# Two-layer diffusion backbone with mixture of experts: the last four expert tiles of layer 0 summed on chip, and the loop over further tiles moved to three tiles from the end

## The chip, the cores and the metric

The kernel runs on one core of one Trainium2 chip. The metric is device time in microseconds (us), the median over runs of one program. The engines are named as in the profile: PE (TensorE, its matmuls), PEld (its weight loads), DVE (VectorE), ACT (ScalarE), POOL (GpSimd), SP (SyncE, which only issues transfers here).

## What is computed

Two layers over 256 latent tokens and 256 context tokens of 1024 numbers each. A layer makes modulation vectors from the conditioning, projects, runs three kinds of attention, projects out, and adds the result with a scaled residual and a layer norm. Then comes the mixture of experts: 32 experts in 4 groups, each token takes the two best experts of its best group:

```python
    out = jnp.zeros_like(h)
    for e in range(N_EXPERTS):
        hidden = jax.nn.silu(h @ w1[e]) * (h @ w3[e])
        out = out + combine[..., e:e + 1] * (hidden @ w2[e])
    return out
...
        x = _ln_affine(ALPHA * x + g2 * _hier_moe(h, w_rg[l], b_rg[l], w_re[l], b_re[l], w1[l], w3[l], w2[l]),
                       ln2_g[l], ln2_b[l])
```

Layer 0 does this for latents and context (512 tokens), layer 1 for the latents alone (256), and its latents are the output.

## The kernel before

**Blocks and tiles.** Tokens lie in blocks of 128 on the partitions: b0 and b1 are the latents, b2 and b3 the context. The experts' work is cut into tiles of 128 token slots: two experts with 64 slots each, or four with 32. Layer 0 has 14 tiles (t0 to t13), layer 1 has 12 (t0 to t11). An expert's weights are three chunks (c = 0, 1, 2) of 1 MiB; the first two hold w1 and w3, the last w2.

**A tile's steps.** `gather` brings the tokens of a tile together by one-hot matmuls (L1179); `up` multiplies by w1 and w3 (L1192), ACT and DVE make the gated product (L1198, L1199); `mid` turns it (L1226). What follows depends on the tile. An away tile does `put`: multiply by w2 (L1237) and write the 128 rows to the HBM tensor `ys` by an SP transfer of 512 KiB. A tile on chip does `back` (L1210 to L1218: which token a slot belongs to, with what weight), `down` (multiply by w2, L1250, evicted at L1258 and L1259, or L1254 to L1256 in layer 1) and `combine` (one-hot matmuls, L1273, added into one accumulator per block by DVE, L1278). In layer 0 the tiles t0 to t12 are away and t13 is on chip; in layer 1 all are on chip.

**The end of layer 0.** After the last `up`, `fold` reads the two rows of every token back from `ys` (8 indirect POOL transfers of 512 KiB, L1465), weighs and adds them (ACT L1469, DVE L1470), multiplies by the gate (L1471) and adds the residual (L1472). Then t13's `combine` is added, and the layer norm (`before`, L414 to L436) and layer 1's projections (L455 to L457, after the transposes L481) follow.

**Weights.** Expert weights come by `dyn_load` (POOL, L142), an indirect transfer that POOL issues; the other loads are issued by SP (L161). `pump` issues the stream's next loads while fewer than `cap` units of 1 MiB are held; a unit comes free when a step has read its chunk. POOL's transfers use eight semaphores in turn (DMASW0 to 7), SP's use eight others (DMAHW0 to 7).

**The loop over further tiles.** A group with more tokens than its slots hold is finished by `rest` (L1478, L1479), a loop on the device whose count `lpi` is read at run time. With these inputs the count is zero in both layers. RP = (1, 1) puts it after the last tile of each layer.

```python
            r = nc.values_load(lpi[0:1, 0:1], min_val=0, max_val=32)
            with tc.For_i(0, r, 1):
```

**Fillers.** The modulation weights of the next layer are multiplied in small steps (`mod_steps`, L320, four matmuls a step), put by `fill` into places where PE would wait; 16 of them belong to layer 1, four at its head, before the transposes, and the others inside its attention.

Of the kernel before, what the change touches and what calls it, by code (L numbers as in the profile page):

```python
# [35 lines left out]
LAG = 2  # L36
FA = (0, 0, 0, 3)
AC = (5, 8)
RP = (1, 1)
LC = (4, 12)  # L40


class Mem:
# [74 lines left out]
def backbone(ctx: ExitStack, tc, ins, out):  # L118
# [64 lines left out]
    def stream_chunk(k, l, c):  # L183
        add((k, l, c), ins["w_in_" + k][l, c], 4 * CH[k])
# [63 lines left out]
    stream_mod(1, 1, 0, 4)  # L248
    for c in range(2):
        stream_chunk("kc", 1, c)  # L250
    for c in range(2, 5):
        stream_b(1, c)
    stream_mod(1, 1, 4, 8)
    for c in range(2):
        stream_chunk("v", 1, c)
    add(("sm", 1), ins["w_small"][1], 1888)
# [121 lines left out]
    def fill(n=1):  # L378
        for _ in range(n):
            if fillers:  # L380
                fillers.pop(0)()
# [77 lines left out]
    def layer(l, first, before=None, after=None):  # L459
        nb = 4 if l == 0 else 2  # L460
        nq = 128 * nb
        last = l == NL - 1
# [6 lines left out]
        tb = mem.get(512)  # L469
        ta = tb.v(2, 2, 2, 64)  # L470

        hT = [[mem.get(UNIT, F32R) for _ in range(2)] for _ in range(2)]
        HT = [[h.v(4, 512) for h in x] for x in hT]

        def turned(items):

# [784 lines left out]

        total = t3("total", 2, 2)

        def combine(par, first=False, final=0):

            OT = oht[par].v(nb, 128)
            YHI, YLO = parts()
            for b in range(nb):
                for f in range(2):
                    fs = slice(f * 512, f * 512 + 512)  # L1270
                    p = bank("a")
                    for i, Y in enumerate((YHI, YLO)):
                        PE.matmul(p, lhsT=OT[:, b, :], rhs=Y[:, f, :], start=(i == 0), stop=(i == 1))  # L1273
                    dst = ACC[b][:, fs]
                    if last and final:
                        V.scalar_tensor_tensor(dst, p, 1.0, dst, op0=OP.mult, op1=OP.add, accum_out=total[:, b, f:f + 1])
                    elif final == 1:
                        V.tensor_tensor(dst, p, BC["g2", b // 2][:, fs], OP.mult)  # L1278
                    elif final:
                        w = scratch()  # L1280
                        V.tensor_tensor(w, p, BC["g2", b // 2][:, fs], OP.mult)
                        V.tensor_tensor(dst, dst, w, OP.add)
                    elif first and not last:
                        S.activation(dst, p, AF.Copy)
                    else:
                        V.tensor_tensor(dst, dst, p, OP.add)

# [167 lines left out]
            for t in range(0 if last else 2):  # L1455
                mod_bcast(l, 5, t, BC["g2", t])

        def fold():

            two = [mem.get(D) for _ in range(nb)]  # L1460
            for b in range(nb):
                acc[b] = mem.get(D)
                ACC[b] = acc[b].v(D)
                for dst, j in ((ACC[b], 0), (two[b].v(D), 1)):
                    G.indirect_dma_start(out=dst, out_offset=None, in_=ys[:, :],  # L1465
                                         in_offset=bass.IndirectOffsetOnAxis(ap=find[:, b, j:j + 1], axis=0),
                                         bounds_check=at_row, oob_is_err=False)
# [5 lines left out]
            for k in two:  # L1473
                k.free()

        def rest(dyn, par, final):

            r = nc.values_load(lpi[0:1, 0:1], min_val=0, max_val=32)  # L1478
            with tc.For_i(0, r, 1):  # L1479
                further(35)  # L1480

                def load(c):
                    if c < 3:
                        dyn_load(dyn, idx[:, NE, c:c + 1])

                load(0)
                onehot(par, [(128, 35)])
                for jj in range(0, 8, 2):
                    gather(par, 1, jj)
                hb = up(par, 0, 1, 128, lambda t, c: dyn, lambda c: load(c + 1))  # L1490
                ws = back(par, 0, 1, 128, 35, par)
                down(mid(hb), ws, 128, lambda t, c: dyn, lambda c: None)
                combine(par, False, final)

        at_rest = len(todo) - RP[l]
        for i, (m, col, e, _, go) in enumerate(todo):
# [11 lines left out]

            def others():
                held = [("exp", l, e + t, 2) for t in range(128 // m)]  # L1510
                rest(slot[held[0]], i % 2 if i < len(todo) - 1 else 0, 2 if i == len(todo) - 1 else 0)
                for k in held:
                    drop(k)
                pump()

            if i == len(todo) - 4:
                cap[0] -= 2
            if i == len(todo) - 1:
                cap[0] = LC[l]
            if i == len(todo) - 2:  # L1520
                xg.pop((qe + 1) % 2).free()
                ohs.pop((qe + 1) % 2).free()
# [12 lines left out]
            hc = None if i < away else mid(hb)  # L1535
            if q < qe:
                for jj in range(4 * at_, 4 * at_ + 4, 2):
                    gather(q + 1, len(sets[q + 1]), jj)
            if i < away:
                put(i, mid(hb), m, W, rel)  # L1540
# [9 lines left out]
        for k in split_y + [iw] + xg + ohs + oht + hh:  # L1550
            k.free()
        cap[0] = 5


        def second(b, xn):
            xn[b] = mem.get(D) if last else acc[b]
            yield from deepnorm(X[b], xn[b].v(D), BC["lg"], BC["lb"], last, 1.0, total[:, b] if last else None)
            if last:
                SP.dma_start(out=out[b * 128:(b + 1) * 128, :], in_=X[b])

        def done():
            for k in bc.values():
                k.free()

        return second, done
# [6 lines left out]
    before, after = layer(0, mod0_steps(0, "e"))  # L1572
    for g in (1, 2):
        fillers.extend(mod_steps(1, g))
    before, after = layer(1, None, before, after)
    together(*[before(b, {}) for b in range(2)])


# [86 lines left out]
```

## Time and profile before

| | before |
|---|---|
| median of 3 runs | 1125.83 us (1125.26 to 1126.35) |
| the profiled execution | 1121.56 us |
| its span in the profile | 1119.8 us |
| PE busy | 1000.2 us, 89% of the span |
| DVE busy | 510.2 us, 46% |
| DMA | 301.06 MB, mean 269 GB/s |
| mean granted PE clock | 0.96 of full speed |

The busy share of PE is a mean over stages. The two expert stages (450 to 607 us in layer 0, 900 to 1096 us in layer 1) move 411 to 420 GB/s, where the highest slice of the page has 423, while PE is nearly full too; between the expert stage of layer 0 and the projections of layer 1 (616 to 656 us) DVE works and PE mostly waits.

### The profile page before, as it was taken

The numbers are of one execution on the slowest core, as the hardware profiler recorded it, in microseconds if no ns is written. First come the engines' busy times: TensorE is split into PE (matmuls) and PEld (weight loads), VectorE is DVE, ScalarE is ACT, GpSimd is POOL, SyncE is SP. The second block draws the span as 40 slices with busy tenths as digits, with TensorE's granted clock in tenths as the row PEclk, the third lists the DMA queues.
The fourth block names the chain that finished last, engine by engine and source line by source line (L and its number), as shares of the span: only waits on it lengthen the run. The fifth ranks groups of instructions, "written<-read, shape, count | busy, mean of one in ns | idle before, by whom it ended". The sixth has DMA issues, their size and how long they took to land. (4 is left out here: it accounts for less than half of the span.)

```text
span 1119.8 us, 14771 instructions
## 1 busy us (share of the span) xinstructions
PE 1000.2 (89%) x5497; PEld 567.9 (51%) x5497; DVE 510.2 (46%) x1369; ACT 347.3 (31%) x707; POOL 303.3 (27%) x326
## 2 busy tenths in 40 slices
PE   4999999999999998999867279999998899999893
PEld 2788744557765553453212158854456554433231
DVE  5644367775575210100001887356665654342244
ACT  4533155553442110111000376134454221211011
POOL 2112134340002412434421222133210045443420
PEclk9999999999999999999999579999998799999997
DMA  9722157420469987899998563356425799999992
GB/s 381 304 73 91 43 207 285 176 76 1 170 272 364 421 357 299 354 422 423 421 421 351 215 221 119 112 201 241 165 76 225 286 363 419 421 421 421 421 421 95
DMA packets 46351, 301.06 MB, mean 269 GB/s; under 512 B 5410, under 2 KB 5794, under 8 KB 14532
## 3 DMA queue, kind: packets, MB, share of 16 engines
q0 software_dynamic: 25824, 177.81, 38.9%
q1 hardware_dynamic: 20452, 122.27, 28.8%
q8 instruction: 45, 0.74, 0.3%
q14 instruction: 30, 0.25, 0.1%
HBM read 292.19 MB, written 7.87 MB: 268 GB/s over the span
## 5 line engine op out<-in xcount | busy, mean ns | idle before, releaser
L142 POOL DMA_INDIRECT u<-in_w_exp,u x162 | 162.0, 1000 | 327.1 <-PE psa L1192 144.0
L1192 PE MATMUL psa<-u,u 128*32 128x512 f32 (+2 forms) x1040 | 221.3, 603 | 16.3 <-DMA u<-in_w_exp,u 16.2
L455 PE MATMUL psa<-u,u 128*128 128x512 f32 (+3 forms) x400 | 141.3, 356 | 1.0 <-ACT u L498 0.7
L456 PE MATMUL psa<-u,u 128*128 128x512 f32 (+3 forms) x400 | 140.4, 352 | 2.0 <-DVE u L450 2.0
L1192 PEld LDWEIGHTS psa<-u,u 128*32 128x32 f32 (+2 forms) x1040 | 65.5, 127 | 146.9 <-issue 109.9
L457 PE MATMUL psa<-u,u 128*128 128x512 f32 (+3 forms) x400 | 139.5, 352 | 0.4 <-DVE u L499 0.3
L1199 DVE TENSOR_TENSOR scr<-scr,psa 128x256 f32<-128x256 f32 x26 | 10.9, 420 | 213.1 <-ACT scr L1198 213.1
L1179 PEld LDWEIGHTS psc<-u,u 128*128 128x128 f32 x640 | 82.7, 197 | 31.5 <-issue 26.5
L878 POOL TENSOR_SCALAR u<-u,ri 128x512 f32<-128x512 f32 (+1 forms) x48 | 68.5, 1431 | 100.2 <-DVE ri L876 82.6
L1179 PE MATMUL psc<-u,u 128*128 128x256 f32 x640 | 92.7, 296 | 3.0 <-DVE u L1165 2.1
L455 PEld LDWEIGHTS psa<-u,u 128*128 128x128 f32 x400 | 75.7, 190 | 12.5 <-ACT u L498 1.1
L456 PEld LDWEIGHTS psa<-u,u 128*128 128x128 f32 x400 | 76.1, 190 | 11.7 <-DVE u L450 3.1
L457 PEld LDWEIGHTS psa<-u,u 128*128 128x128 f32 x400 | 75.6, 190 | 10.0 <-DVE u L499 0.9
L875 ACT ACTIVATE u<-psa,nm 128x512 f32<-128x512 f32 (+1 forms) x96 | 58.4, 615 | 55.8 <-DVE nm L873 50.9
L1198 ACT ACTIVATE scr<-psa 128x256 f32<-128x256 f32 x26 | 10.0, 385 | 192.1 <-PE psa L1192 192.1
L450 DVE TENSOR_TENSOR u<-u,u 128x1024 fp32r<-128x1024 f32 (+4 forms) x38 | 56.2, 1485 | 19.7 <-ACT u L449 19.6
L1237 PE MATMUL pse<-u,scr 128*32 128x512 f32 (+2 forms) x248 | 63.0, 600 | 1.9 <-ACT scr L1227 1.9
L1181 ACT ACTIVATE u<-psc 128x512 f32<-128x512 f32 x52 | 31.1, 597 | 107.9 <-PE psc L1179 69.4
L1250 PE MATMUL pse<-u,scr 128*64 128x512 f32 (+1 forms) x272 | 63.6, 599 | 0.6 <-DMA u<-in_w_exp,u 0.6
L873 DVE TENSOR_REDUCE nm<-psa 128x1 f32<-128x512 f32 (+1 forms) x80 | 53.1, 682 | 14.1 <-PE psa L863 10.5
L419 POOL TENSOR_TENSOR lns<-lns,mhalf 128x1 f32<-128x1 f32 x22 | 14.2, 646 | 149.0 <-DVE lns L418 108.3
L1273 PE MATMUL psa<-u,u 128*128 128x512 f32 x112 | 38.4, 458 | 17.1 <-DVE u L1278 11.0
(315 smaller groups left out, 1360.3 us busy)
## 6 DMA issues: line engine op xcount, KB each, us to landing
u<-in_w_mod SPq DMA_DIRECT2D x48, 1024.0 KB, 5.9
u<-in_w_exp SPq DMA_DIRECT2D x30, 1024.0 KB, 8.0
u<-in_w_out SPq DMA_DIRECT2D x8, 1024.0 KB, 5.0
ys<-u SPq DMA_DIRECT2D x13, 512.0 KB, 8.3
u<-in_w_in_b SPq DMA_DIRECT2D x10, 512.0 KB, 12.4
u<-in_w_in_v SPq DMA_DIRECT2D x4, 960.0 KB, 4.5
u<-in_w_in_qa SPq DMA_DIRECT2D x4, 768.0 KB, 10.4
u<-in_ln_rows SPq DMA_DIRECT2D x6, 512.0 KB, 5.8
```

The costliest lines, as they stand in the source:

```text
L142: G.indirect_dma_start(out=b.ap(UNIT), out_offset=None, in_=wexp_rows, in_offset=bass.IndirectOffsetOnAxis(ap=idx, axis=0), bounds_check=N ...
L450: V.tensor_tensor(l_[:, c], w[:, c], h[:, c].bitcast(F32), OP.subtract)
L455: PE.matmul(p, lhsT=a[0], rhs=b[0], start=first, stop=False)
L456: PE.matmul(p, lhsT=a[0], rhs=b[1], start=False, stop=False)
L457: PE.matmul(p, lhsT=a[1], rhs=b[0], start=False, stop=final)
L873: V.tensor_reduce(out=nm[:, s, 0:n], in_=pv, axis=AX.X, op=OP.max, negate=True)
L875: S.activation(P[:, i, :], pv[:, i, :], AF.Exp, bias=nm[:, s, i:i + 1], accum_out=su[:, s, i:i + 1])
L878: (G if s == 0 else V).tensor_scalar(P[:, i, :], P[:, i, :], ri[:, s, i:i + 1], None, op0=OP.mult)
L1179: PE.matmul(pv[:, j, :], lhsT=H[b][:, k * 128:(k + 1) * 128], rhs=OH[:, b, :], start=(b == 0 and i == 0), stop=(b == nb - 1 and i == 1))
L1192: PE.matmul(g[r, :], lhsT=XG[:, k, at * 128 + r.start:at * 128 + r.stop], rhs=W(t, k // 4).v(4, 512)[:, k % 4, :], start=(k == 0), stop=(k ...
L1237: PE.matmul(y[r, :], lhsT=hc[:, c * 128 + r.start:c * 128 + r.stop], rhs=W(t, 2).v(2, D)[:, c, f * 512:f * 512 + 512], start=(c == 0), sto ...
L1250: PE.matmul(y[r, :], lhsT=hc[:, c * 128 + r.start:c * 128 + r.stop], rhs=W(t, 2).v(2, D)[:, c, f * 512:f * 512 + 512], start=(c == 0), sto ...
```

## The change

HOME = 4 leaves 10 tiles away, so that t10 to t13 of layer 0 do `back`, `down` and `combine`. Reading back is cut in three: `fetch` (the 8 reads) after t10's `up`, `weigh` (weigh and add) after t11's, `fold` (gate and residual) after t13's. RP = (3, 3) puts the loop after t11 of layer 0's 14 tiles and after t9 of layer 1's 12; the tile ahead of it combines at once and keeps its w2 chunks through the loop. HC sets `cap`. The last `combine` is cut into the latents' half and the context's half, with the first step of the latents' layer norm between them. `mod(1,1)` is streamed earlier and eight of its steps stand at the head of layer 1 where there were four.

```diff
-RP = (1, 1)
-LC = (4, 12)
+RP = (3, 3)
+HOME = 4
+HC = (7, 9, 5)
...
-    for k in ("qa", "cq"):
-        for c in range(2):
-            stream_chunk(k, 1, c)
+    for c in range(2):
+        stream_chunk("qa", 1, c)
+    stream_mod(1, 1, 0, 4)
+    for c in range(2):
+        stream_chunk("cq", 1, c)
+    stream_mod(1, 1, 4, 8)
...
-            together(*[before(b, xn) for b in range(2)])
             for c in range(2):
                 presplit("qa", c)
-            fill(4)
+            rest_of([before(b, xn) for b in range(2)])
+            fill(5)
+            make_h()
+            fill(3)
...
-        away = 0 if last else len(todo) - 1
+        away = 0 if last else len(todo) - HOME
...
-        def fold():
-
-            two = [mem.get(D) for _ in range(nb)]
+        two = []
+
+        def fetch():
+
             for b in range(nb):
                 acc[b] = mem.get(D)
                 ACC[b] = acc[b].v(D)
+                two.append(mem.get(D))
                 for dst, j in ((ACC[b], 0), (two[b].v(D), 1)):
                     G.indirect_dma_start(out=dst, out_offset=None, in_=ys[:, :],
                                          in_offset=bass.IndirectOffsetOnAxis(ap=find[:, b, j:j + 1], axis=0),
                                          bounds_check=at_row, oob_is_err=False)
+
+        def weigh():
             for b in range(nb):
                 S.activation(ACC[b], ACC[b], AF.Copy, scale=sc_[:, b, 2:3])
                 V.scalar_tensor_tensor(ACC[b], two[b].v(D), sc_[:, b, 3:4], ACC[b], op0=OP.mult, op1=OP.add)
+            for k in two:
+                k.free()
+
+        def fold():
+
+            for b in range(nb):
                 V.tensor_tensor(ACC[b], ACC[b], BC["g2", b // 2], OP.mult)
                 V.scalar_tensor_tensor(X[b], X[b], ALPHA, ACC[b], op0=OP.mult, op1=OP.add)
...
+            if i == away - 2:
+                cap[0] = HC[0]
+            if last and i == len(todo) - 4:
                 cap[0] -= 2
...
             if i == len(todo) - 2:
...
                 rows()
+                cap[0] = HC[1]
+                pump()
...
-            if i and i - 1 != at_rest and i > away:
-                combine((i - 1) % 2, i == 1)
-            if i == len(todo) - 1 and not last:
+            if i == away and away:
                 for k in yo:
                     k.free()
+                fetch()
+            if i == away + 1 and away:
+                weigh()
+            if i > away and i - 1 != at_rest:
+                combine((i - 1) % 2)
+            if i == len(todo) - 1 and not last:
                 fold()
...
-            if i == at_rest and i < len(todo) - 1:
+            if i == at_rest:
                 combine(i % 2)
                 others()
-        combine((len(todo) - 1) % 2, False, 1)
-        if at_rest == len(todo) - 1:
-            others()
+        par = (len(todo) - 1) % 2
+        finish = [lambda b=b: combine(par, 1, range(b, b + 2)) for b in range(0, nb, 2)]
+        finish[0]()
```

**Where the loop stands on POOL, layer 1.** POOL issues the expert loads. Before, the end of its queue reads as follows: the last four expert loads, two rows of the layer norm's constants, and then the loop (its count is loaded, compared, and the body of three loads is jumped over).

```order
L142 DMA u_8395<-in_w_exp,u_6671 128x2048
L142 DMA u_8487<-in_w_exp,u_6671 128x2048
L142 DMA u_8491<-in_w_exp,u_6671 128x2048
L142 DMA u_8495<-in_w_exp,u_6671 128x2048
L1454 DMA u_8499<-in_ln_rows 128x1024 x2
L1478 TENSOR_LOAD lpi
L1479 COMPARE_AND_BRANCH
```

After the change, with the semaphores that each row waits for: four expert loads, the loop's count and first branch, then (left out here: the body) the row at which the loop is left, and three expert loads behind it.

```order
L143 DMA u_8518<-in_w_exp,u_6802 128x2048 [waits DMASW1_49,PE_49]
L143 DMA u_8522<-in_w_exp,u_6802 128x2048 [waits DMASW2_49,PE_49]
L143 DMA u_8526<-in_w_exp,u_6802 128x2048 [waits DMASW3_49,PE_49]
L1490 TENSOR_LOAD lpi [waits DVE_49]
L1491 COMPARE_AND_BRANCH
...
L1491 UNCONDITIONAL_BRANCH [waits DMASW5_49,DMASW4_49,DMASW6_49,DMASW3_49,DMASW7_49,DMASW2_49,DMAHW0_49,DMASW1_49,DMAHW1_49,DMASW0_49,DMAHW2_49,SP_sequencer_49,DMAHW3_49,DVE_sequencer_49,DMAHW4_49,PE_sequencer_49,DMAHW5_49,Activation_se
L143 DMA u_8795<-in_w_exp,u_6802 128x2048
L143 DMA u_8799<-in_w_exp,u_6802 128x2048
L143 DMA u_8803<-in_w_exp,u_6802 128x2048
L1458 DMA u_8807<-in_ln_rows 128x1024 x2
```

Three expert loads and the constants moved from ahead of the loop to behind it. The row at which the loop is left stands in the same words on all five queues, in both programs; a jump over the body leads there too, and the counts that it waits for are those of every transfer issued ahead of the loop (97 on POOL's eight semaphores in layer 0 of the changed kernel, the three of the body among them).

**Where it stands on PE, layer 1.** Before, the tail of PE's order is t11's last weights' multiplications, t11's `combine` and the loop:

```order
L1250 MATMUL pse<-u_8491,scr 64x512
L1250 MATMUL pse<-u_8495,scr 64x512
L1273 MATMUL psa<-u_6986,u_6987 128x512 x8
L1478 TENSOR_LOAD lpi
L1479 COMPARE_AND_BRANCH
```

After, t9's `down` and `combine` stand ahead of the loop, and all of t10's `up`, whose weights are u_8461 to u_8490, stands behind it:

```order
L1260 MATMUL pse<-u_8379,scr 32x512
L1260 MATMUL pse<-u_8457,scr 32x512
L1283 MATMUL psa<-u_7117,u_7118 128x512 x8
L1490 TENSOR_LOAD lpi
L1491 COMPARE_AND_BRANCH
...
L1491 REGISTER_ALU
L1491 COMPARE_AND_BRANCH
L1491 UNCONDITIONAL_BRANCH
L1202 MATMUL psa<-u_8461,u_7116 64x512
L1202 MATMUL psa<-u_8482,u_7116 64x512
```

Two whole tiles of PE's work (t10 and t11) moved behind the loop; in layer 0 it is t12 and t13.

**DVE at the end of layer 0.** Before, from the last tile's eviction to the loop, DVE weighs (L1470), gates (L1471), adds (L1472) and combines (L1278) in one run, of which this is the end:

```order
L1472 SCALAR_TENSOR_TENSOR u_72<-u_72,u_4713 128x1024
L1471 TENSOR_TENSOR u_4726<-u_4726,u_4611 128x1024
L1278 TENSOR_TENSOR u_4706<-psa,u_3034 128x512
L1472 SCALAR_TENSOR_TENSOR u_72<-u_72,u_4726 128x1024
L1278 TENSOR_TENSOR u_4713<-psa,u_3034 128x512 x2
L1278 TENSOR_TENSOR u_4713<-psa,u_4611 128x512 x2
L1278 TENSOR_TENSOR u_4726<-psa,u_4611 128x512 x2
L1478 TENSOR_LOAD lpi
```

After, between t13's gated product and the layer norm's first instruction (L427) stand t12's combine adds (L1290, eight, the last two shown), the gate and residual (L1485 and L1486, eight, three shown), and t13's combine of the latents:

```order
L1290 TENSOR_TENSOR u_4458<-u_4458,psa 128x512 x2
L1485 TENSOR_TENSOR u_4437<-u_4437,u_4451 128x1024
L1485 TENSOR_TENSOR u_4444<-u_4444,u_4451 128x1024
L1486 SCALAR_TENSOR_TENSOR u_71<-u_71,u_4437 128x1024
...
L1288 TENSOR_TENSOR u_4437<-psa,u_4451 128x512
L452 TENSOR_TENSOR u_5184<-u_4998,u_5183 128x512
L1288 TENSOR_TENSOR u_4437<-psa,u_4451 128x512
L1288 TENSOR_TENSOR u_4444<-psa,u_4451 128x512 x2
L452 TENSOR_TENSOR u_5192<-u_5040,u_5191 128x512 x3
L427 SCALAR_TENSOR_TENSOR u_71,dns<-u_71,u_4437 128x1024
```

The weighing, the loop and the context's combine left this stretch; eight combine adds and six splits of the projection's weights (L452, before: L450, inside the layer norm) came into it.

## Rows read from the trace of the kernel before

**Rows 1.** Windows: stretch, length, busy us (instructions) per engine, PEclk, DMA share, GB/s.

```profile
550.00:607.00 57.00, 42.06 (x151) 12.88 (x150) 5.01 (x15) 4.70 (x10) 11.88 (x12) 0.94 1.01 420
616.00:656.00 40.00, 14.25 (x41) 4.74 (x41) 34.17 (x59) 15.62 (x21) 11.88 (x14) 0.51 0.64 231
740.00:850.00 110.00, 106.54 (x535) 55.18 (x534) 72.82 (x149) 51.74 (x109) 29.43 (x24) 0.98 0.44 154
1064.00:1096.00 32.00, 29.82 (x126) 10.37 (x124) 11.66 (x20) 3.46 (x7) 6.43 (x8) 1.00 0.99 412
```

**Rows 2.** Timeline of POOL, layer 1's last issues: start, us, instruction [idle before, releaser].

```profile
1068.30 0.99 POOL L142 DMA_INDIRECT u<-in_w_exp,u  x1 [1.50 <-PE pse L1250]
1070.79 1.03 POOL L142 DMA_INDIRECT u<-in_w_exp,u  x1 [1.50 <-PE psa L1273]
...
1080.26 0.55 POOL L1454 DMA_DIRECT2D u<-in_ln_rows  x1 [1.65 <-DMA u<-in_w_exp,u]
```

**Rows 3.** Issues in 900 to 1064 us: count, median us to landing.

```profile
u<-in_w_exp,u POOLq DMA_INDIRECT x70, 19.1
```

**Rows 4.** Waits of SP's queue around layer 0's loop: total, times, longest.

```profile
SPq L1479 <- DVEq L1478: 6.2, 1, 6.2
```

**Rows 5.** Chain that ended last, at layer 1's loop: start, us, what.

```profile
1107.01 0.05 DVEq L1479
...
1108.29 0.23 DVE dns L427 x2
```

**Rows 6.** Timeline of DVE, end of layer 1: first instruction behind the loop.

```profile
1108.29 0.23 DVE L427 TENSOR_TENSOR dns<-total 128x1 f32<-128x1 f32 x2 [2.05 <-issue]
```

**Rows 7.** Timeline of DVE, end of layer 0.

```profile
619.91 1.22 DVE L1471 TENSOR_TENSOR u<-u,u 128x1024 f32<-128x1024 f32 x1
...
633.98 3.67 DVE L1278 TENSOR_TENSOR u<-psa,u 128x512 f32<-128x512 f32 x6
639.74 1.22 DVE L425 SCALAR_TENSOR_TENSOR u<-u,u 128x1024 f32<-128x1024 f32 x1 [2.08 <-issue]
...
644.74 0.68 DVE L450 TENSOR_TENSOR u<-u,u 128x512 fp32r<-128x512 f32 x1
```

**Rows 8.** Timeline of PE, last tiles of layer 1.

```profile
1072.37 7.08 PE L1192 MATMUL psa<-u,u 128*64 128x512 f32 x30
1080.38 0.44 PE L1226 MATMUL psa<-ident,scr 128*128 128x128 f32 x2 [0.93 <-DVE scr L1199]
1081.35 3.70 PE L1250 MATMUL pse<-u,scr 128*64 128x512 f32 x16
...
1086.50 2.29 PE L1273 MATMUL psa<-u,u 128*128 128x512 f32 x7 [0.21 <-DVE u L1256]
1088.71 7.08 PE L1192 MATMUL psa<-u,u 128*64 128x512 f32 x30
1096.72 0.44 PE L1226 MATMUL psa<-ident,scr 128*128 128x128 f32 x2 [0.93 <-DVE scr L1199]
```

**Rows 9.** Timeline of PE, `up` of t12 in layer 0.

```profile
581.92 5.34 PE L1192 MATMUL psa<-u,u 128*64 128x512 f32 x14 [2.73 <-DMA u<-in_w_exp,u]
```

**Rows 10.** Timeline of ACT, at the end of t13's `up` in layer 0.

```profile
607.19 0.38 ACT L1198 ACTIVATE scr<-psa 128x256 f32<-128x256 f32 x1 [14.58 <-PE psa L1192]
```

**Rows 11.** Timeline of PE: filler steps, first projection, broadcast of the gate.

```profile
529.35 2.21 PE L390 MATMUL psc<-u,ident 2*128 2x512 f32 x4
...
646.60 1.93 PE L320 MATMUL pse<-u,csil 128*32 128x512 f32 x8 [1.08 <-DMA u<-in_w_mod]
...
659.41 0.42 PE L455 MATMUL psa<-u,u 128*128 128x384 f32 x1
...
751.26 1.06 PE L320 MATMUL pse<-u,csil 128*32 128x512 f32 x8
```

**Rows 12.** Waits of PE in 740 to 850 us: total, times, longest.

```profile
PE pse L908 <- DVE u L897: 2.0, 5, 0.6
```

**Rows 13.** Page, transfers of SP: count, KB each, median us from issue to landing.

```profile
u<-in_w_mod SPq DMA_DIRECT2D x48, 1024.0 KB, 5.9
```

More of the change, by code (lines that the diff above doesn't have):

```diff
@@ L457, in three, with layer @@
         PE.matmul(p, lhsT=a[1], rhs=b[0], start=False, stop=final)
-    def layer(l, first, before=None, after=None):
+    def layer(l, first, before=None, after=None, rest_of=None):
         nb = 4 if l == 0 else 2
@@ L470, in layer, with make_h @@
         ta = tb.v(2, 2, 2, 64)
-        hT = [[mem.get(UNIT, F32R) for _ in range(2)] for _ in range(2)]
-        HT = [[h.v(4, 512) for h in x] for x in hT]
+        hT, HT = [], []
+        def make_h():
+            hT.extend([mem.get(UNIT, F32R) for _ in range(2)] for _ in range(2))
+            HT.extend([h.v(4, 512) for h in x] for x in hT)
+        if not last:
+            make_h()
         def turned(items):
@@ L744, in layer @@
             gains()
-            together(*[before(b, xn) for b in range(2)])
             for c in range(2):
                 presplit("qa", c)
-            fill(4)
+            rest_of([before(b, xn) for b in range(2)])
+            fill(5)
+            make_h()
+            fill(3)
             for j in range(0, 8, 2):
@@ L1262, in layer, with combine @@
         total = t3("total", 2, 2)
-        def combine(par, first=False, final=0):
+        def combine(par, final=0, blocks=range(nb)):
             OT = oht[par].v(nb, 128)
             YHI, YLO = parts()
-            for b in range(nb):
+            for b in blocks:
                 for f in range(2):
@@ L1276, in combine @@
                         V.scalar_tensor_tensor(dst, p, 1.0, dst, op0=OP.mult, op1=OP.add, accum_out=total[:, b, f:f + 1])
-                    elif final == 1:
+                    elif final:
                         V.tensor_tensor(dst, p, BC["g2", b // 2][:, fs], OP.mult)
[L1279 to L1284, printed above, removed]
                     else:
@@ L1470, in fold, with rest @@
                 V.scalar_tensor_tensor(ACC[b], two[b].v(D), sc_[:, b, 3:4], ACC[b], op0=OP.mult, op1=OP.add)
+            for k in two:
+                k.free()
+        def fold():
+            for b in range(nb):
                 V.tensor_tensor(ACC[b], ACC[b], BC["g2", b // 2], OP.mult)
                 V.scalar_tensor_tensor(X[b], X[b], ALPHA, ACC[b], op0=OP.mult, op1=OP.add)
-            for k in two:
-                k.free()
-        def rest(dyn, par, final):
+        def rest(dyn, par, odd):
             r = nc.values_load(lpi[0:1, 0:1], min_val=0, max_val=32)
@@ L1490, in rest @@
                 hb = up(par, 0, 1, 128, lambda t, c: dyn, lambda c: load(c + 1))
-                ws = back(par, 0, 1, 128, 35, par)
+                ws = back(par, 0, 1, 128, 35, odd)
                 down(mid(hb), ws, 128, lambda t, c: dyn, lambda c: None)
-                combine(par, False, final)
+                combine(odd)
         at_rest = len(todo) - RP[l]
@@ L1510, in others @@
                 held = [("exp", l, e + t, 2) for t in range(128 // m)]
-                rest(slot[held[0]], i % 2 if i < len(todo) - 1 else 0, 2 if i == len(todo) - 1 else 0)
+                rest(slot[held[0]], q % 2, i % 2)
                 for k in held:
@@ L1514, in others @@
                 pump()
-            if i == len(todo) - 4:
+            if i == away - 2:
+                cap[0] = HC[0]
+            if last and i == len(todo) - 4:
                 cap[0] -= 2
-            if i == len(todo) - 1:
-                cap[0] = LC[l]
             if i == len(todo) - 2:
-                xg.pop((qe + 1) % 2).free()
-                ohs.pop((qe + 1) % 2).free()
+                for k in hh + [xg.pop((qe + 1) % 2), ohs.pop((qe + 1) % 2)]:
+                    k.free()
                 rows()
+                cap[0] = HC[1]
+                pump()
             if at_ == 0 and q < qe:
@@ L1534, in layer @@
                 lists()
[L1535 to L1538, printed above, removed]
+            pieces = [jj for jj in range(4 * at_, 4 * at_ + 4, 2) if q < qe]
+            if i < away and pieces:
+                gather(q + 1, len(sets[q + 1]), pieces.pop(0))
+            hc = mid(hb)
+            for jj in pieces:
+                gather(q + 1, len(sets[q + 1]), jj)
             if i < away:
-                put(i, mid(hb), m, W, rel)
+                put(i, hc, m, W, rel)
             else:
@@ L1543, in layer @@
                 down(hc, ws, m, W, rel)
-            if i == at_rest and i < len(todo) - 1:
+            if i == at_rest:
                 combine(i % 2)
                 others()
-        combine((len(todo) - 1) % 2, False, 1)
-        if at_rest == len(todo) - 1:
-            others()
-        for k in split_y + [iw] + xg + ohs + oht + hh:
+        par = (len(todo) - 1) % 2
+        finish = [lambda b=b: combine(par, 1, range(b, b + 2)) for b in range(0, nb, 2)]
+        finish[0]()
+        for k in [iw] + xg + ohs + (split_y + oht if last else []):
             k.free()
-        cap[0] = 5
+        cap[0] = HC[2]
         def second(b, xn):
@@ L1559, in second, with rest_of @@
                 SP.dma_start(out=out[b * 128:(b + 1) * 128, :], in_=X[b])
+        def rest_of(steps):
+            steps = list(steps)
+            for g in steps:
+                next(g)
+            if not last:
+                finish[1]()
+                for k in split_y + oht:
+                    k.free()
+            together(*steps)
         def done():
@@ L1563, in done @@
                 k.free()
-        return second, done
+        return second, done, rest_of
     for g in (1, 2):
@@ L1571, in backbone @@
         fillers.append(lambda j=j: (one(j), two(j)))
-    before, after = layer(0, mod0_steps(0, "e"))
+    steps = layer(0, mod0_steps(0, "e"))
     for g in (1, 2):
         fillers.extend(mod_steps(1, g))
-    before, after = layer(1, None, before, after)
-    together(*[before(b, {}) for b in range(2)])
+    before, _, rest_of = layer(1, None, *steps)
+    rest_of([before(b, {}) for b in range(2)])
 def _rope(n_tok, dim):
```

2 lines of the change are left out of this document (removed).

## The prediction

> **What bounds the kernel now.** I read the windows by stage first. In both expert stages the transfers run flat out, 412 to 420 GB/s [rows 1]: before t12 and t13 of layer 0 PE waits for weights, while the late tiles of layer 1 keep PE busy 29.8 of 32 us because POOL is some eight loads ahead of it. The timelines say by how much: an expert load is issued every 2.49 us [rows 2] and lands 19.1 us after its issue [rows 3]. [...] Then PE is the limit again, 106.5 of 110 us in layer 1's attention. So a change here is worth what it does to (1) the run of DVE work that ends layer 0, (2) PE's work in attention, and (3) the last tiles of layer 1, behind which nothing can hide.
>
> **What the loop is.** It runs no pass in either layer, and still no engine gets past it before all have come to it: the SP queue stood at it for 6.2 us until DVE's last instruction was through [rows 4]. The chain of waits shows how it is left: a row of short waits a tenth of a us apart, one of them at 1107.01, and the layer norm only at 1108.29 [rows 5]. The whole gap on DVE is 2.05 us there [rows 6] and 2.08 in layer 0 [rows 7]. The order of the changed program says what these waits are for: the eight semaphores of POOL's transfers, the eight of SP's, and each engine. Before, all transfers have landed when they are reached, so they cost some 2 us. Moved to three tiles from the end, they stand where eight loads are in flight, and every engine must wait until the last load issued ahead of the loop has landed. That is the step on which the forecast rests.
>
> **Layer 1, step by step.** Three expert loads stand behind the loop, so the last one ahead of it is the fourth from the end: in the trace the issue at 1068.30 [rows 2]. Plus 19.1 it lands at 1087.4. A check: the constants' second half can be issued at 1080.26, when the load issued eight before it (three issues ahead of 1068.30) has landed; three more at 2.49 give 1087.7. I take 1087.6. Leaving takes 0.1 (only the last wait open) to 2.05 us; I take 1.1, somewhat under the 1.28 that the chain's rows span [rows 5], so 1088.7. Behind the loop PE has `up` of t10 whole (30 matmuls took 7.08, so 32 take 7.55), 0.93 wait and 0.97 to the start of `down` (1080.38 to 1081.35), 3.70 `down`, 7.55 `up` of t11, and some 2.6 for t10's `combine`, which now stands behind it and covers its wait. That is 23.3, so t11's `mid` begins at 1112.0 at full clock. PE has then stood still since about 1072.4. A much shorter wait, 2.73 us, already cost t12's `up` of layer 0: 14 matmuls in 5.34 [rows 9] where 7.08 for 30 would make 3.30. So I add 2.0 for the clock; the bounds are 0 and 7.5 (all of `up` at half clock). `mid` at 1114.0 stands against 1096.72 before [rows 8], +17.3; the loop at the end is gone, -2.05 [rows 6]. **+15.2, between +12 and +21.** Nothing hides it: the end of the kernel follows `mid` as before.
>
> **Layer 0.** Up to t11's `up` (about 566) only order and `cap` differ, at no cost, since the transfers are full whatever is issued first. The read-back adds 8 times 0.52 MB ahead of the drain, 10.0 us at 420 GB/s; two row writes and a 0.52 MB projection load leave it, -3.7. Before, the weights that t12 waits for land at 581.92 [rows 9], and the one load behind them 2.49 later; plus 6.3 makes 590.7, and out of the loop 591.8. Under that cover lie for nothing the weighing (4 DVE instructions of about 1.2), the 16 combine adds of t10 and t11 (0.61 each [rows 7]) and their added matmuls, since DVE was busy 5.0 and PE 42 of 57 us [rows 1]; with the cover gone the adds and the weighing would be 14.6 us of DVE. Then the gate's broadcasts, one to two groups of four at 2.21 [rows 11], I take 3.3; `up` of t12 7.55 plus 2.0 for the clock; 5.6 to the end of `down`; `up` of t13 7.55, whose weights (five loads, 12.5 us after the exit and some 3 for the first) are there by then. It ends at 617.8 where it ended at 607.19 [rows 10].
>
> From there before took 32.5 us to the layer norm at 639.74. Now DVE has eight adds (4.9), eight gate and residual instructions (1.22 each, 9.8 [rows 7]), back, eviction and the latents' four adds (4.5), and six splits of 0.61 (0.68 alone), 3.7: with gaps 23.5, so 641.3. To the first projection it was 19.7 (659.41 [rows 11]); the splits have gone from there, the context's four adds (2.4) come in, and four more filler steps stand ahead of the transposes on PE, which is mostly idle: 20. First projection at 661.3. **+1.9, between -6 (drain covered, clock full) and +9 (up at half clock, broadcasts and read-back slower).** So the tail's gain of 9 us is eaten by the drain of 10.6.
>
> **Attention.** Four filler steps leave a stretch that is nearly all PE. One step is 1.06 at full clock (1.93 at the lower [rows 11], where the four now go, beside DVE's work); PE waits for softmax 2.0 us in five pieces [rows 12] and may wait where a step stood. **-3, between -4.2 and 0.**
>
> **Sum.** 15.2 + 1.9 - 3 = +14.1 on the profiled execution's 1121.56, 1135.7. The median of the runs lies 4.27 higher, so 1139.9.
>
> **The rivals.** *The loop costs only itself* (ends faster). If the way out did not wait for loads in flight, it would cost its 2 us in a place where PE waits for weights anyway. The bytes ahead of t13's `up` hardly change (4.2 MB of reads, against 1.6 of writes and 2.6 of projection loads that move behind): it would end near 607.5, the tail's 9 us be kept, layer 1 lose 2 and save 2. -9 - 3 = -12, 1114. It decides if t10's `up` in layer 1 follows t9's `combine` within 3 us. Against it: the SP queue's 6.2 us and the chain's waits. [...] 7 in 100.
>
> *Layer 0 pays.* The drain there falls into waits for weights, which t12 and t13 had anyway, and DVE's tail shrinks fully: the far end of layer 0's bounds, -6, with -4 in attention and the low end of layer 1, +12 to +14. +2 to +4, up to +8. For it: PE's free 15 us of 57 in that stage. Against: what lies behind the drain, two tiles of `up`, `mid` and `down`, is PE work that no longer overlaps the transfers ahead. 20 in 100.
>
> *Late modulation weights.* SP too stands at the loop, so no weight of layer 1 is on its way before 591.8, and all eight filler steps stand ahead of the transposes. The last two of those loads wait on SP's queue behind a load whose buffer the splits free, at about 641; they land 5.9 us [rows 13] and 2.5 later, by 650, just before the transposes. If they come 8 us later, the first projection does: +22, up to +30. 15 in 100.
>
> **How the numbers follow.** The forecast, +8 to +18 with +14 likeliest, has 58 in 100, and these three 42. A difference of 0.2% (2.25 us) is about what can be told from none. Faster by more is the first rival and a trace of the second, 8 in 100; within it, the bottom of the second, 4; slower 88. From +2.5 to +23.5, 1128.3 to 1149.3, lies the forecast with most of the second rival and half of the third, 8 in 10.
>
> **What would show it.** In the changed profile, layer 1: no matmul on PE between t9's `combine` (about 1072, shifted by what layer 0 brings) and some 16 us later, transfers full to the end of that gap and then empty for a few us, a lower clock in the `up` behind it. Layer 0: the same gap before the broadcasts at about 592, the layer norm some 23 us after t13's `up`. At the end: no 2 us gap ahead of the last layer norm. The forecast is wrong if POOL's last three loads are issued less than 10 us after the ones ahead of the loop, or if the gap is filled.

## The result, and the profile after

| | before | after |
|---|---|---|
| median | 1125.55 us (1123.67 to 1126.58, 6 runs) | 1136.85 us (1132.56 to 1138.38, 6 runs) |
| ratio of the runs | | 1.0095, 95% interval 1.0075 to 1.0116 |
| span of the profiled execution | 1119.8 us | 1134.1 us |
| mean granted PE clock | 0.960 | 0.954 |

The changed kernel is slower by 11.3 us in the medians and by 14.3 in the profiled executions. The windows of [rows 1], asked again of the changed kernel (stretch, length, busy us and instructions of PE, PEld, DVE, ACT and POOL, then PE clock, DMA share and GB/s):

```profile
550.00:607.00 57.00, 44.84 (x158) 17.23 (x156) 22.98 (x53) 9.96 (x14) 21.44 (x21) 0.79 0.91 366
616.00:656.00 40.00, 29.22 (x150) 13.33 (x146) 33.27 (x53) 8.55 (x15) 4.93 (x7) 0.91 0.76 302
740.00:850.00 110.00, 107.59 (x548) 60.77 (x547) 75.22 (x164) 53.33 (x112) 32.17 (x27) 1.00 0.37 132
1064.00:1096.00 32.00, 13.62 (x53) 4.53 (x53) 5.27 (x8) 1.26 (x2) 6.90 (x8) 0.73 0.82 331
```

In the last row PE has lost 16.2 of its 29.8 busy us, and the transfers run at 331 GB/s instead of 412. PE's timeline there (start, us, instruction, idle before and its releaser) shows one hole, and behind it a slower `up`:

```profile
1070.61 1.88 PE L1283 MATMUL psa<-u,u 128*128 128x512 f32 x7 [1.01 <-DVE u L1266]
1089.29 9.32 PE L1202 MATMUL psa<-u,u 128*64 128x512 f32 x32 [16.80 <-issue]
...
1110.97 2.12 PE L1283 MATMUL psa<-u,u 128*128 128x512 f32 x8
1112.93 0.38 PE L1236 MATMUL psa<-ident,scr 128*128 128x128 f32 x2
```

"issue" as releaser means that the profile sees nothing that PE waited for; in the order of the changed program the waits stand on the branch ahead of it (L1491). The chain of waits (start, us, what) names what was late:

```profile
1068.75 19.07 DMA u<-in_w_exp,u
1087.82 1.47 issue
1089.29 9.35 PE psa L1202 x32
```

The load issued at 1068.75 is the last one ahead of the loop; it lands at 1087.82, and 1.47 us later PE goes on. POOL's timeline has the same gap, with the issue that answers to [rows 2] ahead of it:

```profile
1068.75 0.99 POOL L143 DMA_INDIRECT u<-in_w_exp,u  x1 [1.49 <-PE pse L1260]
1089.69 0.99 POOL L143 DMA_INDIRECT u<-in_w_exp,u  x1 [19.95 <-issue]
```

In layer 0 the hole is in the transfers as well. The rate in 40 slices of 580 to 610 us, 0.75 us each:

```profile
GB/s 404 437 426 404 437 377 442 431 421 437 393 426 437 426 284 98 76 0 0 0 0 22 120 109 382 426 382 251 295 328 328 426 404 437 404 426 426 415 459 399
```

SP's queue waited there (total, times, longest):

```profile
SPq L1491 <- DMA u<-in_w_exp,u: 13.8, 1, 13.8
```

The rate falls from 590.5 on and is nothing from 592.8 to 595.8; the full rate is back at 598. SP had issued its last transfer by 579.3 and waited 13.8 us, to 593.1. DVE's timeline tells what else had to end:

```profile
585.82 5.09 DVE L1290 TENSOR_TENSOR u<-u,psa 128x512 f32<-128x512 f32 x8
594.81 0.38 DVE L1406 MEMSET capv<- 128x2 f32 x12 [3.90 <-issue]
...
646.13 1.22 DVE L427 SCALAR_TENSOR_TENSOR u<-u,u 128x1024 f32<-128x1024 f32 x1
```

PE's timeline shows what stands behind the loop:

```profile
595.13 2.08 PE L392 MATMUL psc<-u,ident 2*128 2x512 f32 x4 [5.82 <-issue]
...
599.99 9.92 PE L1202 MATMUL psa<-u,u 128*64 128x512 f32 x32
...
653.79 1.06 PE L322 MATMUL pse<-u,csil 128*32 128x512 f32 x8 [2.06 <-DMA u<-in_w_mod]
...
669.39 0.67 PE L457 MATMUL psa<-u,u 128*128 128x384 f32 x1
```

t11's eight combine adds end at 590.91, some 2 us ahead of the last landing; the loop is left at 594.8. PE stands idle for 5.82 us, then does the gate's broadcasts (L392), and t12's `up` begins at 600.0. `up` of t13 ends at 622.73 (607.19 before [rows 10]), the layer norm begins at 646.13 (639.74 [rows 7]) and the first projection at 669.39 (659.41 [rows 11]).

### The profile page after: what moved, and what is told of

Same layout as the page of the kernel before. It is cut to its first block, busy times and chain, and to the rows that moved or that the text cites. A ratio compares the mean times of both kernels' runs of the same rounds, so it can differ in the third digit from the quotient of the medians.

```text
span 1134.1 us, 14960 instructions
## 1 busy us (share of the span) xinstructions
PE 1010.3 (89%) x5581; PEld 582.6 (51%) x5581; DVE 530.0 (47%) x1402; ACT 350.5 (31%) x710; POOL 302.7 (27%) x323
## 5 line engine op out<-in xcount | busy, mean ns | idle before, releaser
L1202 PE MATMUL psa<-u,u 128*32 128x512 f32 (+2 forms) x1040 | 217.1, 606 | 23.5 <-issue 16.8
L458 PEld LDWEIGHTS psa<-u,u 128*128 128x128 f32 x400 | 76.8, 192 | 11.6 <-DVE u L452 3.1
L457 PEld LDWEIGHTS psa<-u,u 128*128 128x128 f32 x400 | 76.7, 192 | 11.3 <-ACT u L506 1.1
L459 PEld LDWEIGHTS psa<-u,u 128*128 128x128 f32 x400 | 76.3, 192 | 9.5 <-issue 0.8
L1260 PE MATMUL pse<-u,scr 128*64 128x512 f32 (+1 forms) x320 | 78.9, 609 | 0.6 <-DMA u<-in_w_exp,u 0.6
L452 DVE TENSOR_TENSOR u<-u,u 128x1024 fp32r<-128x1024 f32 (+4 forms) x38 | 56.1, 1486 | 20.4 <-ACT u L451 20.3
L1283 PE MATMUL psa<-u,u 128*128 128x512 f32 x160 | 50.5, 442 | 14.1 <-ACT u L1268 7.4
L421 POOL TENSOR_TENSOR lns<-lns,mhalf 128x1 f32<-128x1 f32 x22 | 15.2, 693 | 172.4 <-DVE lns L420 172.1
L1247 PE MATMUL pse<-u,scr 128*32 128x512 f32 (+2 forms) x200 | 53.8, 600 | 1.5 <-ACT scr L1237 0.9
```

Of the source, the lines that this page charges most:

```text
L452: V.tensor_tensor(l_[:, c], w[:, c], h[:, c].bitcast(F32), OP.subtract)
L457: PE.matmul(p, lhsT=a[0], rhs=b[0], start=first, stop=False)
L1202: PE.matmul(g[r, :], lhsT=XG[:, k, at * 128 + r.start:at * 128 + r.stop], rhs=W(t, k // 4).v(4, 512)[:, k % 4, :], start=(k == 0), stop=(k ...
L1247: PE.matmul(y[r, :], lhsT=hc[:, c * 128 + r.start:c * 128 + r.stop], rhs=W(t, 2).v(2, D)[:, c, f * 512:f * 512 + 512], start=(c == 0), sto ...
L1260: PE.matmul(y[r, :], lhsT=hc[:, c * 128 + r.start:c * 128 + r.stop], rhs=W(t, 2).v(2, D)[:, c, f * 512:f * 512 + 512], start=(c == 0), sto ...
```

## The experiments

The theory is that the loop is the price: it can be left only when every transfer issued ahead of it has landed. The rivals are that other parts of the change cost the time, that a loop has a fixed price, or that the two loops' delays are one. Each run was timed beside the kernel before, and the ratio and its 95% interval are to that. The changed kernel was not timed again: "less than the changed kernel" is the difference of two such differences (11.3 us for the changed kernel), each of which is known to 2 to 4 us either way.

**1. The loop's move alone, in the kernel before.**

```diff
-RP = (1, 1)
+RP = (1, 3)
```

> The kernel before with one part of the change alone: the loop of layer 1 three tiles from the end (RP = (1, 3)). Drain theory: the loop is left when the last load issued ahead of it has landed, so PE stands still from t9's combine (about 1072) to about 1089, and the kernel takes 12 to 15 us more than before (span 1132 to 1135). Rival, the loss is in the other parts (read-back traffic and combine adds in layer 0, order of loads): within 2 us of before.

Measured: 1137.33 us against 1124.01, ratio 1.0110 (1.0076 to 1.0143), span 1134.6. PE's timeline has the hole:

```profile
1070.93 1.90 PE L1273 MATMUL psa<-u,u 128*128 128x512 f32 x7 [1.00 <-DVE u L1256]
1089.62 9.51 PE L1192 MATMUL psa<-u,u 128*64 128x512 f32 x32 [16.79 <-issue]
```

One line of the change gives 13.3 us, as much as the whole change (11.3). The rival that other parts cost the time falls; that they are worth 2 us together is within the intervals.

**2 and 3. The changed kernel without one loop.** In 2 the loop of layer 1 is left out, in 3 that of layer 0 (with `if last:`).

```diff
             if i == at_rest:
                 combine(i % 2)
-                others()
+                if not last:
+                    others()
+                else:
+                    for t in range(128 // m):
+                        drop(("exp", l, e + t, 2))
+                    pump()
```

> The changed kernel with layer 1's loop left out (it runs no pass on these inputs; the device could not serve further tiles in that layer). Drain theory: PE's gap of 16.8 us ahead of t10's up is gone, t11's mid begins near 1097 instead of 1112.9, the span is 1117 to 1120, 14 to 17 us under the changed kernel. Rival, other parts: 0 to 2 us under it.

Measured: 1121.61 us against 1124.01, ratio 0.9977 (0.9961 to 0.9994), so 13.7 us less than the changed kernel by the differences to the kernel before. `up` of t10 follows t9's `combine` at once, and `mid` of t11 comes at 1101.76:

```profile
1077.39 7.09 PE L1202 MATMUL psa<-u,u 128*64 128x512 f32 x32
...
1101.76 0.44 PE L1236 MATMUL psa<-ident,scr 128*128 128x128 f32 x2 [0.93 <-DVE scr L1209]
```

The span, 1123.0, misses the expected 1117 to 1120, since this execution came to layer 1's experts 4.5 us later (880.14 against 875.68), with the same program up to there. From its start of the experts to its end it took 15.6 us less than the changed kernel.

> The changed kernel with layer 0's loop left out. Drain theory: no hole in the transfers at 587 to 597, t12's up begins when DVE has freed t11's combine (about 590 instead of 600.0), t13's up ends near 612 instead of 622.7, the first projection near 659 instead of 669.9; the kernel is 8 to 12 us faster than the changed one. Rival, the loop there hides behind DVE's adds and the weights: 0 to 4 us faster.

Measured: 1122.43 us against 1124.01, ratio 0.9983 (0.9964 to 1.0001), span 1117.2: 12.9 us less than the changed kernel. The transfers have no hole (the same 40 slices of 580 to 610 us):

```profile
GB/s 448 415 421 388 459 371 448 404 448 404 448 415 404 459 382 426 393 437 426 415 426 415 437 415 404 429 423 401 423 423 423 410 426 396 437 421 434 426 404 437
```

On PE's timeline the broadcasts stand ahead of t11's `down`, `up` of t12 begins at 592.02 and the first projection at 652.32:

```profile
575.81 2.07 PE L392 MATMUL psc<-u,ident 2*128 2x512 f32 x2 [0.35 <-ACT u L394]
...
592.02 7.09 PE L1202 MATMUL psa<-u,u 128*64 128x512 f32 x32
...
652.32 0.67 PE L457 MATMUL psa<-u,u 128*128 128x384 f32 x1
```

That is 7 us earlier than in the kernel before and 17.1 earlier than in the changed one, more than was expected (659). On the way there it was less: `up` of t13 ended at 618.65, only 4.1 us earlier than in the changed kernel and not near 612. But DVE ran the gate and residual instructions while PE still worked on it, so that the layer norm began at 630.71 instead of 646.13, 12.1 us behind `up` and not 23.4. Without the loop the order on DVE and PE itself comes out differently. So layer 0's price is not the hole alone.

**4. Layer 1's loop one tile later**, after t10 (the buffers of the gathered tokens' source are freed behind the loop; the lines for this are left out here).

```diff
-RP = (3, 3)
+RP = (3, 2)
```

> The changed kernel with layer 1's loop one tile later, after t10 (RP = (3, 2)). Drain theory: what counts is when the last load ahead lands; all expert loads are then ahead of it and land near 1096, so t11's up begins near 1097, its mid near 1108: 3 to 7 us faster than the changed kernel. Rival, a fixed price of a loop in mid-stream (16.8 us wherever it stands): t11's mid near 1115, no faster than the changed kernel.

Measured: 1132.55 us against 1124.01, ratio 1.0077 (1.0047 to 1.0107), 2.8 us less than the changed kernel; span 1128.3. By the intervals the 2.8 us could be nothing; the trace tells more. The hole is shorter and ends where the last load lands. POOL's last expert load, and PE's `up` of t11 behind the loop, from their timelines:

```profile
1074.38 0.99 POOL L143 DMA_INDIRECT u<-in_w_exp,u  x1 [1.51 <-DMA u<-in_w_exp,u]
```

```profile
1097.11 9.47 PE L1202 MATMUL psa<-u,u 128*64 128x512 f32 x32 [10.10 <-issue]
```

Behind that load POOL issued the constants in two halves of 512 KiB, and the chain of waits has the second one's landing and the way out:

```profile
1078.87 17.09 DMA u<-in_ln_rows
1095.95 1.16 issue
1097.11 9.50 PE psa L1202 x32
```

A fixed price would have made the hole 16.8 us again and put `mid` of t11 at 1115; the hole was 10.10, and `mid` came at 1107.52 (this execution was some 2 us ahead of the changed kernel's at t9's `combine`). The price is the time until the last landing.

**5. Neither loop** (the branch of runs 2 and 3, in both layers).

> The changed kernel with the loop left out in both layers (it runs no pass on these inputs; further tiles could not be served). Drain theory: the two prices add, 13 to 15 us in layer 1 and 13 to 15 in layer 0, so 26 to 30 us under the changed kernel, 14 to 18 us under the kernel before (span 1101 to 1106). Rival, the two prices are one delay counted twice (once the first is gone, PE's slack hides the second): no more than 18 us under the changed kernel.

Measured: 1105.64 us against 1124.88, ratio 0.9836 (0.9810 to 0.9862), span 1103.7: 30.5 us less than the changed kernel, where 2 and 3 give 26.6 together. The two prices add. Everything else in the change is worth 19.2 us to the good, though this kernel also has no loop at a layer's end, which is some 4 us of that by the 2.05 and 2.08 us of [rows 6] and [rows 7].

**6. Both loops at the end of their layer**, with all tokens served.

```diff
-RP = (3, 3)
+RP = (1, 1)
...
-            if i == at_rest:
+            if i == at_rest and RP[l] > 1:
                 combine(i % 2)
                 others()
...
         finish[0]()
+        if RP[l] == 1:
+            if not last:
+                finish[1]()
+            others(1 if last else 2)
+            for k in hh:
+                k.free()
```

> The changed kernel with both loops after the last combine of their layer, as in the kernel before (RP = (1, 1); the gathered tokens' buffers are held until then, and in layer 0 both halves of the last combine stand ahead of the loop). Drain theory: nothing but layer 1's first weights is in flight there, each loop costs 2 to 6 us again, first projection at 656 to 662 (669.9 in the changed kernel, 659.4 before), span 1108 to 1114, 6 to 12 us under the kernel before. Rival, a loop with the changed kernel's larger code costs more wherever it stands: no faster than the kernel before.

Measured: 1117.04 us against 1124.88, ratio 0.9932 (0.9910 to 0.9954), span 1117.8, faster than both kernels. The span and the first projection (666.0) miss the expected 1108 to 1114 and 656 to 662; some 2 us of it is this execution, which was 2.3 us behind the changed kernel's when PE's order was still the same (an `up` at 506.67 against 504.37). At the head of layer 1 PE leaves the loop and runs into weights that SP could issue only behind it:

```profile
640.90 4.50 PE L322 MATMUL pse<-u,csil 128*32 128x512 f32 x40 [2.20 <-DVEq L1495]
650.19 1.93 PE L322 MATMUL pse<-u,csil 128*32 128x512 f32 x8 [4.79 <-DMA u<-in_w_mod]
```

The loads of those weights were issued only after SP had stood at the loop for 4.6 us and then waited 3.0 us for DVE's splits (L452). So at the end of layer 0 the loop costs 2 us by itself (2.20 on PE here) and holds back loads.

**7. Four filler steps at the head, in the changed kernel.**

```diff
-            fill(5)
+            fill(4)
             make_h()
-            fill(3)
```

> The changed kernel with four filler steps at the head of layer 1 as before, so that four more stand inside attention. If the steps are what attention gained (its part from first to last scores took 71.9 us before and 62.5 after), that part takes 69 to 73 us and the kernel is 5 to 9 us slower than the changed one. Rival, attention gained by the reordered loads and splits: 0 to 3 us slower.

Measured: 1140.13 us against 1124.88, ratio 1.0136 (1.0109 to 1.0164), 3.9 us more than the changed kernel, between the two forecasts. It does not test what it was made for. The order on PE has the matmuls of all eight steps ahead of the transposes as before the edit; only the four transposes that end them (L371) moved into attention. Attention still has eight steps, cut into 12 pieces instead of 10, and its part took 67.5 us instead of 62.5. The matmuls of these pieces were busy for 12.68 us instead of 10.60, so two more pieces are 2.1 of the 5 us; the rest was not taken apart. The question went to run 8.

**8. The filler part alone, in the kernel before**, with the modulation weights streamed as in the changed kernel.

```diff
-            fill(4)
+            fill(8)
```

> The kernel before with one part of the change alone: eight filler steps at the head of layer 1 instead of four, and the modulation weights streamed as in the changed kernel. If the steps are what attention gained, the part from first to last scores takes 62 to 66 us instead of 71.9 (and ten pieces of a filler step stand there, not 16), while the first projection moves from 659.4 to 660 to 667, because four more steps and their weights stand ahead of it: between 2 us slower and 8 us faster than before. Rival, attention gained by other work of the change: part within 3 us of 71.9, and the kernel 0 to 8 us slower than before.

Measured: 1121.01 us against 1123.79, ratio 0.9977 (0.9958 to 0.9995). The part from first to last scores took 62.5 us (71.9 before). Its ends on PE's timeline, in the kernel before:

```profile
746.17 1.12 PE L863 MATMUL psa<-u 64*128 64x512 f32 x2
...
816.23 1.88 PE L863 MATMUL psa<-u 96*128 96x512 f32 x4
```

In this kernel:

```profile
749.80 1.12 PE L864 MATMUL psa<-u 64*128 64x512 f32 x2
...
810.45 1.88 PE L864 MATMUL psa<-u,u 96*128 96x512 f32 x4
```

The first projection began at 663.11, 3.7 later than before. Windows give the busy time of the filler line alone in 740 to 830 us (stretch, length, PE and PEld with their rows, two to a matmul, then clock, DMA share, GB/s). The kernel before:

```profile
740.00:830.00 90.00, 16.93 (x94) 2.40 (x94) 1.00 0.50 175
```

This kernel:

```profile
740.00:830.00 90.00, 10.60 (x64) 1.52 (x64) 0.98 0.39 139
```

The changed kernel:

```profile
740.00:830.00 90.00, 10.60 (x64) 1.52 (x64) 1.00 0.41 147
```

6.3 us of the 9.4 is PE's time on the steps. The run moves the order of the loads together with the steps, so it does not part the two by itself; but PE waited for no load in this part in any of the three kernels, and run 7, with the changed kernel's loads and 12 pieces, stands between (67.5).

**9. Layer 1's loop at the end, layer 0's where the change has it** (with the other lines of run 6).

```diff
-RP = (3, 3)
+RP = (3, 1)
```

> The changed kernel with layer 1's loop after its last combine, layer 0's loop left where the change put it (RP = (3, 1)); all tokens can be served. Drain theory: the kernel without layer 1's loop took 2.4 us less than the kernel before; the loop at the end adds 2.1: within 2 us of the kernel before. Rival, the loop costs as much at the end, since the gathered tokens' buffers are held longer and fewer weights are prefetched: 5 us or more slower than before.

Measured: 1123.38 us against 1123.79, ratio 0.9995 (0.9979 to 1.0012), as expected. Moving this one loop back undoes the whole loss of the change.

**10. Both loops at the end, and a shorter head of layer 1** (shown against run 6).

```diff
+    stream_mod(1, 1, 0, 8)
     for c in range(2):
         stream_chunk("cq", 1, c)
-    stream_mod(1, 1, 4, 8)
...
+            rest_of([before(b, xn) for b in range(2)])
             for c in range(2):
                 presplit("qa", c)
-            rest_of([before(b, xn) for b in range(2)])
```

> Both loops at the end of their layer as in the kernel that took 7.8 us less than before, and two edits at the head of layer 1: all eight modulation weights streamed ahead of the cq chunks, and the splits of the projection's weights after the first step of the layer norm instead of ahead of it. There the layer norm took 16.3 us from its first instruction to the normalised block, 11.9 in the kernel before, with six splits in it. If splits and late weights hold the head, first projection at 661 to 664 instead of 666.0 and 2 to 5 us faster than that kernel. Rival, the chain of the layer norm over DVE, ACT and POOL holds it: within 1.5 us.

Measured: 1112.36 us against 1123.79, ratio 0.9901 (0.9874 to 0.9929), span 1109.8, the fastest kernel here that serves all tokens. By the differences to the kernel before that is 3.6 us less than run 6, as forecast, though the two intervals meet. The head was shorter: from the loop's end (PE at 634.74) the first projection took 21.1 us (655.87), against 25 in run 6. That the loop was left 6 us earlier (640.90 in run 6) is not the edits' doing for the most part: PE's order is the same up to there, 4.4 us of the six stand already at t12's `mid` (602.11 against 606.55), and t13's `down` took 3.70 us against 5.37, with a mean granted clock of 0.972 in this execution against 0.961 in run 6's. Two edits went in together, and what each gave was not separated.

## Why the prediction was right

The time, 1136.85 us, lies in the range (1128.3 to 1149.3), 3 us under the forecast of 1139.9. The sum for the profiled execution, +14.1, met the span's +14.3. That it met so closely is luck: of its three terms one was right (layer 1, within 1.5 us), and two lay outside their bounds, 8.1 us too low (layer 0) and 6.4 us too high (attention).

**The drain** is shown by runs 1, 2, 4 and 9. The last load ahead of the loop was expected to land at 1087.6 and landed at 1087.82. Leaving took 1.47 us, where 1.1 was taken.

**Layer 1, +15.2.** `up` of t10 began at 1089.29 (1088.7 expected), took 9.32 us (9.55 expected, 2.0 of it for the clock, which was granted at 0.50 in 1089 to 1092 us, when PE came back), and `mid` of t11 began at 1112.93 (1114.0). Less the loop at the end and 0.4 us by which t9 came later, that is 13.7, the figure that run 2 gives in medians. Moving the loop alone cost 13.3.

**Layer 0, +1.9, between -6 and +9: mis-sized, it was +10.0**, outside its bounds. Three steps of the sum failed. First, the drain ended at about 593 and not 590.7, and the loop was left at 594.8 and not 591.8: the transfers were full until 590.5, and the last of them came in at a falling rate (284, 98 and 76 GB/s in the last three slices). Second, the broadcasts took 4.9 us with their copies, not 3.3. Third, the head of layer 1 took 23.3 us instead of 20. The tail in between was right: 23.4 us from `up` to the layer norm, with the six splits in it, 23.5 expected.

The combine adds and the weighing were to lie under the drain for nothing, and they filled it nearly to its end. They held PE's combine of t10 back (waits of 1.89 and 0.99 us), the granted clock was 0.58 in 570 to 580 us where the 10 us before had 1.00, t11's `down` took 6.48 us where the one in [rows 8] took 3.70, and t11's adds ended at 590.91. The window of 570 to 580 us (engines as above, clock 0.58) and the `down`:

```profile
570.00:580.00 10.00, 7.87 (x26) 4.18 (x28) 9.11 (x13) 3.44 (x4) 4.68 (x5) 0.58 1.03 419
```

```profile
577.86 6.48 PE L1260 MATMUL pse<-u,scr 128*64 128x512 f32 x16
```

So without the loop `up` of t12 began only at 592.0 (run 3). The 8 us to the changed kernel's 600.0 are PE's hole of 5.8 and the broadcasts of 4.9 behind it, less 2.8 by which t11's `combine` ended later in run 3, since there the broadcasts stand ahead of it. At the end of t13's `up` 4.1 of the 8 are left; most of what run 3 gave lies in the tail behind (12.1 us instead of 23.4), where DVE's order is another than with the loop, and not in the wait.

In the head PE waited for modulation weights in two places (2.06 and 1.62 us), as the third rival said, and then the transposes ran at half clock (granted 0.50 in 658 to 670 us). ACT waited for them too, for longer than PE: a split of weights (L451) stands ahead of the layer norm's second pass (L418) in ACT's order, and it came when PE's last filler step was through:

```profile
651.04 0.19 ACT L418 ACTIVATION_READ_ACCUMULATOR scr<-u,lns 128x1 f32 x1
658.06 1.06 ACT L451 ACTIVATE u<-u 128x1024 fp32r<-128x1024 f32 x1 [6.84 <-PE pse L322]
659.03 1.13 ACT L418 ACTIVATE u<-u,lns 128x1024 f32<-128x1024 f32 x1
```

DVE had the input of that pass ready at 657.9, so this order cost the layer norm about 1.2 us (an estimate from these rows).

**Attention, -3, between -4.2 and 0: mis-sized, it was -9.4** in the part from first to last scores (71.9 to 62.5). Runs 7 and 8 put it down to the steps. A step was priced at 1.06 us, the row of an undivided one. Where the order cuts a step's four matmuls in two, each piece took as long as the whole (1.04 to 1.07 us in these runs, for one matmul as for four): 16 pieces became 10, which is 6.3 us on PE by the busy times. The other 3 us were not taken apart; one group of the transposes that end the steps (0.66 us) is in them.

**The rivals.** That the loop costs only itself falls with run 1, where the hole is 16.79 us; it ends with a landing (the changed kernel, 1.47 us after it, and run 4, 1.16). That layer 0 pays fell the other way: without the loop it would have paid, 7 us against the kernel before at the first projection (run 3); with it, it lost 10. Late modulation weights cost 3.7 us of PE's waits and ACT's 1.2 behind them, not 8.

So where did the gain of the change go? Runs 5 and 6 show it: without the loops' move the rest of the change is worth 8 us (both loops at the layers' ends), and with no loops at all about 19; the move of two loops of no passes turns this into a loss.

## What to carry to other kernels

In these programs a loop on the device with a count from the data is a place where all engines and all transfers in flight meet, also when it runs no pass (PE stood at it for 16.80 us with loads in flight, and for 2.20 at the end of layer 0 in run 6); the order of a program shows whether its loop is left by such waits. Put it where the queues are empty anyway, or price it at the landing of the last load issued ahead of it (1087.82 in the changed kernel, PE at work again at 1089.29) plus the work that PE has left behind it. Other work moves behind it with the loop, as the broadcasts did in layer 0 (4.9 us). When small matmuls are moved as fillers, count the pieces they are cut into, not the steps (1.04 to 1.07 us a piece here).

## What the runs showed that was not expected

- A filler step's four matmuls of 32 columns took 1.06 us together, and each of the two pieces 1.04 to 1.06 when the order cut the step: 16 pieces had 16.93 us, 10 had 10.60.
- PE's clock fell while PE was busy 7.87 of 10 us (570 to 580 us in the changed kernel, mean granted clock 0.58), in a stretch where its combine waited for DVE's adds.
- Executions with the same order of instructions up to a place came to it up to 4.5 us apart (start of layer 1's experts at 875.68 in the changed kernel and 880.14 in run 2), more than several of the differences asked about here. Some 3 us of this arose at one place: in 834 to 840 us the projection's matmuls began every 0.43 us in run 2 and every 0.23 in the changed kernel (mean granted clock of 820 to 850 us 0.89 and 1.00), while PE was busy throughout in both.
